# Convolution input, queries and gate of a hybrid RG-LRU and attention layer: from still to moving weights, turned by TensorE, with two attention lanes and a new order of column groups

## The chip, the cores and the metric

The kernel runs on one core of one Trainium2 chip. The metric is device time in microseconds (us), the median of several runs; lower is better. The engines named below are PE (TensorE: matrix products, with its weight loads as PEld), ACT (ScalarE), DVE (VectorE), POOL (GpSimd) and SP, whose queue issues the loads of the weights.

## The reference

One layer on 256 tokens of 2048 channels, all in float32:

```python
h = h + W_out [ norm(RG-LRU group) ; norm(NSA group) ]   # one RMSNorm, one combined input projection
h = h + ConvGatedMLP(RMSNorm(h))                          # then a final RMSNorm
# columns of the input projection w_in (2048 x 4632)
C_X, C_G, C_Q, C_KC, C_VC, C_KS, C_VS, C_KW, C_VW, C_BG = (
    0, 1024, 2048, 3072, 3328, 3584, 3840, 4096, 4352, 4608)
```

X (1024 columns) goes through a causal convolution of 4 taps to `u`; two products of `u` with 128x128 blocks per head give the gates r and i (sigmoids); with a = exp(-8 r softplus(-lambda)) the recurrence is h_t = a_t h_(t-1) + sqrt(1 - a_t^2) i_t u_t, and its result is multiplied by gelu(G), G being 1024 columns more. Q, K and V serve an attention of 8 query heads and 2 key heads with three branches: over compressed blocks (a small two-layer network with weights `cmp_w1` on K and V), over selected blocks, over a window. Both halves are normed and go through `w_out`.

## The kernel before

**Products.** Each float32 product is three products of the faster fp32r type: a weight is split into hi + lo, the activations too, and hi·hi, hi·lo and lo·hi are summed in PSUM. The weights stream through in parts of 128 x 1024 numbers (`PART`), two to a load of 1 MB on SP's queue (tile `raw`, 3 buffers). For each part ACT makes `hi` (L285) and DVE makes `lo` (L286); each of the two pools has 4 buffers. All that PE does for a part takes some 2.7 to 2.9 us.

**Three ways to multiply.** `mm_weights_still_plain` (L314) loads 128x128 of the weight into PE and moves 256 tokens through it, three matmuls of 256 columns (L323 to L325); the result has channels on partitions. `mm_weights_still` (L328) moves the activations' hi and lo side by side, 512 columns, for the weight's hi (L345) and 256 columns for its lo (L343); `halves` then adds the two halves of the result. `mm_weights_move` (L357) loads 128 tokens of the activations and moves up to 512 columns of the weight (L369 to L371); the result has tokens on partitions.

**Order.** `run_stream` (L290) walks a list of parts. The list is made of column groups: KC and VC by turns, KS, KW by turns with `cmp_w1_k`, Q's first 256 columns by turns with `cmp_w1_v`, then VW, Q, VS, Q, Q, four groups of 256 for X, four for G, four of 512 for `w_out` with the attention half, four with the LRU half, and then `w_up`, the convolution and `w_down` in three pieces. All of X, G, Q and K use `mm_weights_still_plain`. The code beside the products hangs in lanes (`Lane`, L57): each is a queue of generators, run whenever its due time has come, where the clock is counted in matrix steps (`PACE` a step of 256 columns). The tile framework then sets the order of each engine's queue.

**What the lanes do.** `norm_x` (L379) makes the scale of the first norm and then `blocks` (L425): the blocks of K and V for compression, on POOL (L427, L434), split by ACT (L436) and DVE (L437) into `kbs`. `post_q` (L508) scales the queries and adds two `attention` tasks, for tokens 0 to 127 and 128 to 255, to one lane. `post_lru_x` writes X to `xp`, and `lru` (L664) does convolution, gate products (L694 to L696) and tanh/exp for a pair of heads (ACT L698 to L702). When the last G group is done `recurrence` (L716) takes square roots (L725), scans (DVE L731), gelu of G (L734) and the product (L737), split for `w_out` by `two_parts` (L216).

Of the kernel before, what the change touches and what calls it, by code (L numbers as in the profile page):

```python
# [15 lines left out]
P = 128  # L16
# [62 lines left out]
def hymba_block(ctx, tc, x, g_mix, w_in, lru_conv_w, lru_conv_b, lru_wa, lru_ba, lru_wx, lru_bx, lru_lambda,  # L79
# [43 lines left out]
    mix = mixctx.enter_context(tc.tile_pool(name="mix", bufs=1))  # L123
    cmpp = cmpctx.enter_context(tc.tile_pool(name="cmpp", bufs=1))
# [91 lines left out]
    def two_parts(dst, src, gain=None):  # L216

        hi, lo = dst[:, 0], dst[:, 1]
        if gain is None:
            act(hi, src, AF.Copy)  # L220
            tt(lo, src, hi.bitcast(F32), op=OP.subtract)
        else:
            act(hi, src, AF.Copy, scale=gain)  # L223
            stt(lo, src, gain, hi.bitcast(F32), op0=OP.mult, op1=OP.subtract)  # L224

    def transpose_in(cg, g, dst):

        for pair in range(2):
            t = ps_t.tile([P, 512], F32, name="pt")
            for j in range(2):  # L230
                c = cg * 512 + (pair * 2 + j) * P
                for b in range(NB):
                    nc.tensor.transpose(t[:, j * S + b * P:j * S + (b + 1) * P], xr[:, b, c:c + P], ident)
            for j in range(2):
                i = pair * 2 + j
                two_parts(dst[:, i], t[:, j * S:(j + 1) * S], g(cg * 4 + i))
# [11 lines left out]
    lanes = {n: Lane() for n in ("x", "att", "lru", "gate")}  # L248
# [65 lines left out]
    def mm_weights_still_plain(src):  # L314

        def fn(p, j, k, st, kts):
            if k == 0:
                st["ps"] = ps_mm.tile([P, 2, 512], F32, name="mm")
            a = src(k)
            for m in range(2):  # L320
                o = st["ps"][:, m, :S]
                wh, wl = p.hi[:, j, m * P:(m + 1) * P], p.lo[:, j, m * P:(m + 1) * P]
                mm(o, lhsT=wh, rhs=a[:, 0], start=k == 0, stop=False)  # L323
                mm(o, lhsT=wh, rhs=a[:, 1], start=False, stop=False)  # L324
                mm(o, lhsT=wl, rhs=a[:, 0], start=False, stop=k == kts - 1)  # L325
        return fn

# [20 lines left out]
    def halves(dst, ps):  # L348

        t = ev.tile([P, 2, S], F32, name="ev")  # L350
        nc.scalar.copy(t, ps[:, :, S:])  # L351
        tt(dst, ps[:, :, :S], t, op=OP.add)  # L352

# [28 lines left out]
    def norm_x():  # L382
# [12 lines left out]
        rsq = cst.tile([P, S], F32, name="rsbq")  # L395
        nc.vector.tensor_scalar_mul(rsq, shared["rsb"], QSCALE)
        shared["rsbq"] = rsq
# [3 lines left out]
        blocks(0)  # L401
        yield 1000
        blocks(1)
# [13 lines left out]
    kbs = [cmpp.tile([P, CB, 2, KVH * NC], F32R, name=f"kbs{i}") for i in range(2)]  # L417
    NST = 4 * KVH * NC

    def post_cmp_in(which):  # L420
        def post(st):
            nc.vector.tensor_copy(kvc[:, which], st["ps"][:, :, :S])
        return post

    def blocks(which):  # L425

        nc.gpsimd.tensor_tensor(kvc[:, which], kvc[:, which], over_pair(shared["rsb"]), op=OP.mult)  # L427
        src = kvc[:, which].rearrange("p v (n l) -> p l v n", l=CS)
        kb = cmpp.tile([P, CB, KVH * NC], F32, name="kb")
        dst = kb.rearrange("p l (v n) -> p l v n", v=KVH)  # L430
        for half in range(2):
            for v in range(KVH):
                off = pe[:, which * CB + half * CS:which * CB + (half + 1) * CS]
                nc.gpsimd.tensor_tensor(dst[:, half * CS:(half + 1) * CS, v], src[:, :, v, half:half + NC],  # L434
                                        off.unsqueeze(2).to_broadcast([P, CS, NC]), op=OP.add)
        act(kbs[which][:, :, 0], kb, AF.Copy)  # L436
        tt(kbs[which][:, :, 1], kb, kbs[which][:, :, 0].bitcast(F32), op=OP.subtract)  # L437

# [15 lines left out]
    def post_cmp(which):  # L454
# [5 lines left out]
        def finish_cmp(ps):  # L460
# [15 lines left out]
            else:  # L476
# [7 lines left out]
                open_mixers()  # L484
        return post

    def post_keys(br):
        def post(st):
            tt(kcat[:, :, br], st["ps"][:, :, :S], over_pair(shared["rsb"]), op=OP.mult)
        return post  # L490

    ready = set()

    def post_values(br):
        def post(st):
            ready.add(br)
            for b in range(NB):
                src, rs = st["ps"][:, b, :256], shared["rs"][:, b:b + 1]
                act(vnat[0][:, b, br], src, AF.Copy, scale=rs)
                stt(vnat[1][:, b, br], src, rs, vnat[0][:, b, br].bitcast(F32), op0=OP.mult, op1=OP.subtract)  # L500
            if br == 1:

                for b in range(NB):
                    act(gates[:, b], st["ps"][:, b, 256:280], AF.Tanh, scale=shared["rsh"][:, b:b + 1])
                ts(gates, gates, 0.5, 0.5, op0=OP.mult, op1=OP.add)
        return post

    def post_q(i):  # L508
        def post(st):
            tt(qT[:, 2 * i:2 * i + 2], st["ps"][:, :, :S], over_pair(shared["rsbq"]), op=OP.mult)  # L510
            if i % 2 == 1:
                yA.append(split_new())
                for b in range(NB):
                    lanes["att"].add(attention(i // 2, b))
        return post

# [8 lines left out]
    def open_mixers():  # L525
        late["at"] = mixctx.enter_context(tc.tile_pool(name="at", bufs=1))
        late["lr"] = mixctx.enter_context(tc.tile_pool(name="lr", bufs=1))
# [23 lines left out]
    def attention(g, b):  # L551
# [13 lines left out]
        pc = at.tile([P, GQA, NC], F32, name="pc")  # L565
# [11 lines left out]
        pr = at.tile([P, GQA, 2, S], F32, name="pr")  # L577
# [13 lines left out]
        yield 1000  # L591
        nc.vector.reciprocal(cf, tot)
# [19 lines left out]
        for n, step in enumerate(steps):  # L612
# [5 lines left out]
            pT = [at.tile([P, 512], F32R, name=f"pT{n % 2}{i}") for i in range(2)]  # L618
# [8 lines left out]
        sq = at.tile([P, 512], F32R, name="pT00").bitcast(F32)  # L627
        act(sq, o, AF.Square)
        for h in range(GQA):
            two_parts(yA[g][:, h, :, qs], o[:, h * P:(h + 1) * P], g_att(g * GQA + h))  # L630
# [21 lines left out]
    lru_sq = cst.tile([P, S], F32, name="lru_sq")  # L652
    halfway = []
    gated = []

    def post_lru_x(i):
        def post(st):
            xp = late["lr"].tile([P, 2, S + 3], F32, name="xp")
            nc.gpsimd.memset(xp[:, :, 0:3], 0.0)
            tt(xp[:, :, 3:], st["ps"][:, :, :S], over_pair(shared["rsb"]), op=OP.mult)  # L660
            lanes["lru"].add(lru(i, xp))
        return post

    def lru(i, xp):  # L664
        lr = late["lr"]
# [6 lines left out]
        e = lr.tile([P, 2, S], F32, name=f"gt{i}")  # L672
# [7 lines left out]
        for m in range(2):  # L680
            t = 2 * i + m
            nc.gpsimd.tensor_scalar(u[:, m], xp[:, m, 0:S], conv_w(0, t), conv_b(t), op0=OP.mult, op1=OP.add)
# [25 lines left out]
    def post_lru_g(i):  # L708
        def post(st):
            gt = late["lr"].tile([P, 2, S], F32, name=f"gt{i}")  # L710
            tt(gt, st["ps"][:, :, :S], over_pair(shared["rsb"]), op=OP.mult)
            gated.append(gt)
            if i == 3:
                lanes["lru"].add(recurrence())
        return post

    def recurrence():
        room = scratch_new()
        ms = [room[:, :, h] for h in range(2)]
        for m, w in zip(ms, halfway):  # L720
            stt(m, w[:, :, 0], 2.0, w[:, :, 0], op0=OP.subtract, op1=OP.mult)
            nc.gpsimd.tensor_scalar(w[:, :, 0], w[:, :, 0], -1.0, 1.0, op0=OP.mult, op1=OP.add)
        yield 2600
        for m in ms:
            act(m, m, AF.Sqrt, scale=-0.25)  # L725
        yield 1500
        for m, w in zip(ms, halfway):
            tt(w[:, :, 1], w[:, :, 1], m, op=OP.mult)
            yield 1500
            for j in range(4):  # L730
                nc.vector.tensor_tensor_scan(m[:, j], w[:, j, 0], w[:, j, 1], 0.0, op0=OP.mult, op1=OP.add)  # L731
            yield 2000
        for gt in gated:
            act(gt, gt, AF.Gelu_apprx_tanh)  # L734
        yield 2000
        for i, gt in enumerate(gated):
            tt(gt, gt, ms[i // 2][:, (i % 2) * 2:(i % 2) * 2 + 2], op=OP.mult)  # L737
            if i % 2 == 0:
                yL.append(split_new())
            for m in range(2):  # L740
                two_parts(yL[i // 2][:, (i % 2) * 2 + m], gt[:, m], g_lru(2 * i + m))
            yield 1500
            for m in range(2):
                if i == 0 and m == 0:
                    nc.gpsimd.tensor_tensor(lru_sq, gt[:, 0], gt[:, 0], op=OP.mult)
                else:
                    nc.gpsimd.tensor_tensor(gt[:, m], gt[:, m], gt[:, m], op=OP.mult)
                    nc.gpsimd.tensor_tensor(lru_sq, lru_sq, gt[:, m], op=OP.add)
            yield 1000
        yield 5000  # L750
        shared["rsL"] = channel_rms(lru_sq, "rsL")
# [50 lines left out]
    def post_up_v(t0):  # L802
        def post(st):
# [7 lines left out]
            two_parts(aT[t0 // 4][:, i % 4:i % 4 + 2].rearrange("p k a s -> p a k s"), v)  # L811
# [74 lines left out]
    group(wi, C_KS, 256, KT, still_x, post_keys(0))  # L886
    with_cmp = lambda g, w, which: by_turns(g, group(w[0], 0, P, CB, mm_cmp(which), post_cmp(which), cuts=[8] * (CB // 8)))
    with_cmp(group(wi, C_KW, 256, KT, still_x, post_keys(1), cuts=halves_of), cmp_w1_k, 0)
    still_q = lambda i, cuts=None: group(wi, C_Q + i * 256, 256, KT, still_x, post_q(i), cuts=cuts)
    with_cmp(still_q(0, halves_of), cmp_w1_v, 1)  # L890
    group(wi, C_VW, 280, KT, move_x, post_values(1))
    still_q(1)
    group(wi, C_VS, 256, KT, move_x, post_values(0))
    still_q(2)
    still_q(3)
    for i in range(4):
# [50 lines left out]
```

## Time and profile before

| | |
|---|---|
| median of 3 runs | 1178.77 us (1178.74 to 1179.24) |
| profiled execution, its own time | 1178.34 us |
| span in its trace | 1176.6 us, so 1.74 us lie outside it |
| busy: PE, DVE, ACT, POOL | 1160.9, 778.6, 589.7, 159.8 us |
| chain that ended last: PE, DVE | 91%, 2% |
| input projection and mixers | about the first 280 of the 1176.6 us |

Busy times say how long an engine was at work in all; the chain follows back from the last instruction what released each step. Matmuls overlap one another on PE, so their step from start to start is what one costs, and not the duration of one.

### The profile page before, as it was taken

The numbers are of one execution on the slowest core, as the hardware profiler recorded it, in microseconds if no ns is written. First come the engines' busy times: TensorE is split into PE (matmuls) and PEld (weight loads), VectorE is DVE, ScalarE is ACT, GpSimd is POOL, SyncE is SP. The second block draws the span as 40 slices with busy tenths as digits, with TensorE's granted clock in tenths as the row PEclk, the third lists the DMA queues.
The fourth block names the chain that finished last, engine by engine and source line by source line (L and its number), as shares of the span: only waits on it lengthen the run. The fifth ranks groups of instructions, "written<-read, shape, count | busy, mean of one in ns | idle before, by whom it ended". The sixth has DMA issues, their size and how long they took to land.

```text
span 1176.6 us, 16684 instructions
## 1 busy us (share of the span) xinstructions
PE 1160.9 (99%) x6727; PEld 1021.8 (87%) x6727; DVE 778.6 (66%) x981; ACT 589.7 (50%) x803; POOL 159.8 (14%) x181
## 2 busy tenths in 40 slices
PE   8999999999999999999999999999999999999997
PEld 7999999898788888888888888888888888888885
DVE  5775778779766676677455676677455677677554
ACT  5554546687446554444333455444333445445444
POOL 3210224123300110110000110110000110110000
PEclk8999999999999999999999999999999999999999
DMA  9676545443655565565555565565555565565561
GB/s 297 180 222 215 159 126 156 135 150 139 214 191 177 176 206 181 180 210 184 188 205 181 181 210 181 179 203 190 184 209 180 179 210 183 179 198 189 189 207 76
DMA packets 182397, 217.60 MB, mean 185 GB/s; under 512 B 4064, under 2 KB 147584, under 8 KB 182192
## 3 DMA queue, kind: packets, MB, share of 16 engines
q1 hardware_dynamic: 180928, 213.07, 55.4%
q0 software_dynamic: 1072, 2.41, 0.6%
q8 instruction: 52, 0.85, 0.4%
q10 hardware_dynamic: 320, 1.06, 0.2%
q14 instruction: 25, 0.20, 0.1%
HBM read 214.43 MB, written 2.10 MB: 184 GB/s over the span
## 4 chain that ended last, share of the span: by engine, by line
PE 91%; DVE 2%; ACT 0%; issue 0%; POOL 0%; DVEq 0%
PE mm L345 30%; PE mm L343 16%; PE mm L370 9%; PE mm L371 9%; PE mm L369 9%; PE mm L325 4%; PE mm L323 4%; PE mm L324 4%; PE s L582 1%; DVE lo L286 1%; PE s L371 1%; PE s L369 1%; PE s L370 1%; PE pt L617 1%; DVE act L224 0%; PE s L608 0%
## 5 line engine op out<-in xcount | busy, mean ns | idle before, releaser
L286 DVE TENSOR_TENSOR lo<-raw,hi 128x1024 fp32r<-128x1024 f32 (+1 forms) x403 | 527.6, 1316 | 248.2 <-ACT hi L285 248.1
L285 ACT ACTIVATE hi<-raw 128x1024 fp32r<-128x1024 f32 (+1 forms) x403 | 423.9, 1054 | 397.0 <-PE mm L371 183.4
L345 PE MATMUL mm<-act,hi 128*128 128x512 f32 x1536 | 367.7, 391 | 0.0
L345 PEld LDWEIGHTS mm<-act,hi 128*128 128x128 f32 x1536 | 282.1, 188 | 54.3
L370 PE MATMUL mm<-lo,act 128*128 128x512 f32 (+2 forms) x544 | 206.0, 379 | 2.1 <-DVE lo L286 2.1
L371 PE MATMUL mm<-hi,act 128*128 128x512 f32 (+2 forms) x544 | 205.7, 378 | 0.0
L369 PE MATMUL mm<-hi,act 128*128 128x512 f32 (+2 forms) x544 | 205.6, 378 | 0.0
L343 PEld LDWEIGHTS mm<-act,lo 128*128 128x128 f32 x1536 | 197.3, 191 | 7.7
L343 PE MATMUL mm<-act,lo 128*128 128x256 f32 x1536 | 199.8, 283 | 0.0
L323 PE MATMUL mm<-act,hi 128*128 128x256 f32 x512 | 147.1, 290 | 2.5 <-ACT act L223 1.7
L325 PE MATMUL mm<-act,lo 128*128 128x256 f32 x512 | 147.8, 289 | 0.1
L324 PE MATMUL mm<-act,hi 128*128 128x256 f32 x512 | 146.8, 288 | 0.4 <-DVE act L224 0.4
L370 PEld LDWEIGHTS mm<-lo,act 128*128 128x128 f32 x544 | 102.2, 188 | 22.4 <-DVE lo L286 3.8
L369 PEld LDWEIGHTS mm<-hi,act 128*128 128x128 f32 x544 | 102.2, 188 | 19.0 <-issue 0.4
L371 PEld LDWEIGHTS mm<-hi,act 128*128 128x128 f32 x544 | 102.2, 188 | 18.8
L356 POOL TENSOR_TENSOR up<-up,rsb 128x512 f32<-128x512 f32 x24 | 29.6, 1234 | 587.7 <-DVE up L352 503.6
L323 PEld LDWEIGHTS mm<-act,hi 128*128 128x128 f32 x512 | 98.3, 193 | 5.4 <-issue 2.1
L325 PEld LDWEIGHTS mm<-act,lo 128*128 128x128 f32 x512 | 98.7, 193 | 2.8 <-issue 1.8
L324 PEld LDWEIGHTS mm<-act,hi 128*128 128x128 f32 x512 | 98.7, 193 | 2.2 <-issue 1.2
L351 ACT COPY ev<-mm 128x512 f32<-128x512 f32 x48 | 28.2, 587 | 125.8 <-PE mm L345 125.8
L352 DVE TENSOR_TENSOR up<-mm,ev 128x512 f32<-128x512 f32 x24 | 16.6, 692 | 49.5 <-ACT ev L351 49.5
L356 POOL TENSOR_TENSOR cv<-cv,rsb 128x512 f32<-128x512 f32 x24 | 38.0, 1582 | 20.8 <-ACT cv L797 20.8
(238 smaller groups left out, 737.9 us busy)
## 6 DMA issues: line engine op xcount, KB each, us to landing
raw<-in_w_up_dram SPq DMA_DIRECT2D x96, 1024.0 KB, 5.2
raw<-in_w_down_dram SPq DMA_DIRECT2D x48, 1024.0 KB, 5.1
raw<-in_w_in_dram SPq DMA_DIRECT2D x26, 1024.0 KB, 5.5
raw<-in_w_out_dram SPq DMA_DIRECT2D x16, 1024.0 KB, 5.0
raw<-in_w_in_dram SPq DMA_DIRECT2D x15, 512.0 KB, 4.6
xr<-in_x_dram SPq DMA_DIRECT2D x4, 512.0 KB, 7.6
raw<-in_cmp_w_k_dram SPq DMA_DIRECT2D x4, 512.0 KB, 5.7
raw<-in_cmp_w_v_dram SPq DMA_DIRECT2D x4, 512.0 KB, 5.4
```

The source lines that it names most:

```text
L285: act(hi[:, :n], src, AF.Copy)
L286: tt(lo[:, :n], src, hi[:, :n].bitcast(F32), op=OP.subtract)
L323: mm(o, lhsT=wh, rhs=a[:, 0], start=k == 0, stop=False)
L324: mm(o, lhsT=wh, rhs=a[:, 1], start=False, stop=False)
L325: mm(o, lhsT=wl, rhs=a[:, 0], start=False, stop=k == kts - 1)
L343: mm(o[:, S:], lhsT=w, rhs=a[:, 0], start=False, stop=False)
L345: mm(o, lhsT=w, rhs=a.rearrange("p a s -> p (a s)"), start=kk == 0, stop=kk == kts - 1)
L351: nc.scalar.copy(t, ps[:, :, S:])
L356: nc.gpsimd.tensor_tensor(a, a, over_pair(shared[rs]), op=OP.mult)
L369: keep(mm(o, lhsT=h, rhs=p.hi[:, j], start=k == 0, stop=False))
L370: mm(o, lhsT=h, rhs=p.lo[:, j], start=False, stop=False)
L371: mm(o, lhsT=l, rhs=p.hi[:, j], start=False, stop=k == kts - 1)
```

## The change

It has five parts. (1) `mm_weights_still_plain` is gone: KC, VC, KS and KW use `mm_weights_still`, with `halves` behind it. (2) X, Q and G are six groups of 512 columns with the weights moving. Their results have tokens on partitions, so ACT copies them to `tok` with the norm's scale (`by_token`), and PE turns them back with 128x128 transposes (`turned`), 8 to a group. (3) The two attention tasks of a group of heads run in two lanes (`att0`, `att1`). (4) The group order is KC/VC, X0, KS with `cmp_w1_k`, KW with `cmp_w1_v`, Q0, VW, VS, Q1, X1, G0, G1, then `w_out` as before. (5) `blocks` runs on DVE; the LRU's first convolution tap and the sign change of the recurrence move from POOL to ACT; the pool `lr` has one buffer of each tile (`tok`, `xp`, `u`, ...), which `recurrence` and `gate` take over from `lru`; square roots are done for each pair and gelu reads the transposes from PSUM.

```diff
-    still_x, move_x = mm_weights_still_plain(tiles_of(xT)), mm_weights_move(tiles_of(xT))
+    still_x, move_x = mm_weights_still(tiles_of(xT)), mm_weights_move(tiles_of(xT))
...
-        nc.gpsimd.tensor_tensor(kvc[:, which], kvc[:, which], over_pair(shared["rsb"]), op=OP.mult)
+        tt(kvc[:, which], kvc[:, which], over_pair(shared["rsb"]), op=OP.mult)
...
+    def by_token(st, rs):
+        tok = lr.tile([P, NB, 512], F32, name="tok")
+        for b in range(NB):
+            act(tok[:, b], st["ps"][:, b], AF.Copy, scale=shared[rs][:, b:b + 1])
+        return tok
+    def turned(tok, pair):
+        t = ps_t.tile([P, 512], F32, name="pt")
+        for j in range(2):
+            c = (pair * 2 + j) * P
+            for b in range(NB):
+                nc.tensor.transpose(t[:, j * S + b * P:j * S + (b + 1) * P], tok[:, b, c:c + P], ident)
+        return t.rearrange("p (j s) -> p j s", j=2)
...
+    def recurrence():
+        room = [lr.tile([P, 2, S], F32, name="u")]
...
+            act(w[:, :, 0], w[:, :, 0], AF.Identity, scale=-1.0, bias=1.0)
+            yield 700
+        for m in room:
+            act(m, m, AF.Sqrt, scale=-0.25)
...
+    def gate(cg, tok):
+        while len(scanned) < 4:
+            yield PACE
+        yield 1300
+        turns = [turned(tok, pair) for pair in range(2)]
...
+        for gt, t in zip(gts, turns):
+            act(gt, t, AF.Gelu_apprx_tanh)
...
-    group(wi, C_KS, 256, KT, still_x, post_keys(0))
+    wide = lambda c0, post: group(wi, c0, 512, KT, move_x, post)
+    wide(C_X, post_lru_x(0))
+    with_cmp(group(wi, C_KS, 256, KT, still_x, post_keys(0), cuts=halves_of), cmp_w1_k, 0)
...
-    for i in range(4):
-        group(wi, C_G + i * 256, 256, KT, still_x, post_lru_g(i))
+    wide(C_X + 512, post_lru_x(1))
+    for cg in range(2):
+        wide(C_G + cg * 512, post_lru_g(cg))
```

Three places show how the change moves instructions. The first is ACT's queue at the beginning of `w_out`. Before, it holds the last splits (`hi`), the gelu of G (L734), the two square roots (L725), and then a run of splits:

```order
L285 ACTIVATE hi<-raw 128x1024
L734 ACT_TABLE_LOAD
L734 ACTIVATE gt_3187<-gt_3187 128x512
L285 ACTIVATE hi<-raw 128x1024
L725 ACT_TABLE_LOAD
L725 ACTIVATE act<-act 128x4x256 x2
L285 ACTIVATE hi<-raw 128x1024 x4
```

At the same place of the queue after the change the square roots (L748) and the gelu (L765) alternate with the last pair's exp and tanh (L726, L727), each with a load of the function table; `wg` and `u` are the taken-over buffers, L745 is the sign change, L493 the copy of the second G group to `tok`:

```order
L748 ACT_TABLE_LOAD
L748 ACTIVATE u_2495<-u_2495 128x512
L727 ACT_TABLE_LOAD
L727 ACTIVATE act<-act,sp_591 128x256
L286 ACTIVATE hi<-raw 128x1024
L726 ACTIVATE xp<-act,sp4n 128x256
L745 ACTIVATE act<-act 128x2x256
L748 ACT_TABLE_LOAD
L748 ACTIVATE u_2494<-u_2494 128x512
L765 ACT_TABLE_LOAD
L765 ACTIVATE wg_2621<-pt 128x512
L493 ACTIVATE tok<-mm,rs 128x512 x2
```

From the split of the fourth `w_out` part to that of the ninth, 5 splits now share ACT's queue with 8 table loads; before, the last square roots stand ahead of a run of 4 splits.

The second place is PE's queue where G1 ends and `w_out` begins (L361 to L363 are the moving matmuls, L719 to L721 the gate products of the third pair of heads, L502 the transposes of the fourth). After the change:

```order
L719 MATMUL pt<-u_2244,wg_2246 128x256
L720 MATMUL pt<-u_2245,wg_2246 128x256
L721 MATMUL pt<-u_2244,wg_2247 128x256
L502 MATMUL pt<-ident,tok 128x128 x4
L665 MATMUL pt<-ones,att_sq 128x1 x2
L361 MATMUL mm<-hi,act 128x512
L362 MATMUL mm<-lo,act 128x512
L363 MATMUL mm<-hi,act 128x512
```

The fourth pair of heads is turned only here, just ahead of the first matmul of `w_out`; the fourth pair's gate products and both G tiles' transposes follow among the `w_out` parts.

The third place is the making of the blocks for compression. Before, it is on POOL:

```order
L427 TENSOR_TENSOR kvc<-kvc,rsb 128x512 x2
L434 TENSOR_TENSOR kb<-kvc,pe 128x16x15 x8
```

After the change it is in DVE's queue between the splits (L287):

```order
L419 TENSOR_TENSOR kvc<-kvc,rsb 128x512 x2
L427 TENSOR_TENSOR kb<-kvc,pe 128x16x15 x4
L287 TENSOR_TENSOR lo<-raw,hi 128x1024 x2
L433 TENSOR_TENSOR act<-kb,act 128x32x30
L427 TENSOR_TENSOR kb<-kvc,pe 128x16x15 x4
```

The blocks left POOL's queue, and the eight X0 parts now lie between KC/VC and the first use of the blocks.

## Rows read from the trace of the kernel before

**Rows 1.** The page: its span, busy times, and the chain by engine

```profile
span 1176.6 us, 16684 instructions
...
PE 1160.9 (99%) x6727; PEld 1021.8 (87%) x6727; DVE 778.6 (66%) x981; ACT 589.7 (50%) x803; POOL 159.8 (14%) x181
...
PE 91%; DVE 2%; ACT 0%; issue 0%; POOL 0%; DVEq 0%
```

**Rows 2.** Windows: us, busy PE, PEld, DVE, ACT, POOL, granted clock, DMA share, GB/s

```profile
371.20:1176.60 805.40, 796.93 (x4237) 689.48 (x4235) 513.90 (x569) 372.06 (x439) 78.00 (x76) 1.00 0.56 186
...
238.00:272.00 34.00, 34.00 (x267) 32.36 (x267) 25.50 (x42) 29.29 (x45) 5.58 (x10) 1.00 0.55 181
272.00:300.00 28.00, 26.11 (x131) 20.86 (x130) 28.00 (x33) 16.42 (x22) 13.72 (x15) 1.00 0.34 119
```

**Rows 3.** Waits of PE over the span: total us, times, longest us

```profile
PE mm L370 <- DVE lo L286: 2.1, 4, 0.9
...
PE mm L323 <- ACT hi L285: 0.8, 1, 0.8
PE s L450 <- ACT hi L285: 0.4, 1, 0.4
```

**Rows 4.** Timeline of DVE from 276 us: start us, us, instruction

```profile
277.29 4.75 DVE L731 TENSOR_TENSOR_SCAN act<-act 128x256 f32<-128x256 f32 x8
281.96 1.20 DVE L286 TENSOR_TENSOR lo<-raw,hi 128x1024 fp32r<-128x1024 f32 x1
```

**Rows 5.** The chain in 59 to 70 us: start us, us, what

```profile
63.00 2.35 POOL kb L434 x2
...
65.37 1.03 ACT kbs L436
```

**Rows 6.** The chain at 269, 341 and 387 us: start us, us, what

```profile
269.93 0.12 PE mm L324
...
272.93 0.12 PE mm L325
...
341.53 0.66 PE pt L233 x6
...
387.46 3.67 PE mm L345 x16
391.13 1.91 PE mm L343 x16
```

**Rows 7.** Timeline of PE at 280 and 341 us: start us, us, instruction

```profile
280.18 0.39 PE L370 MATMUL mm<-lo,act 128*128 128x512 f32 x1
...
282.68 0.39 PE L369 MATMUL mm<-hi,act 128*128 128x512 f32 x1
...
341.94 0.48 PE L369 MATMUL mm<-hi,act 128*128 128x512 f32 x1
```

**Rows 8.** Timeline of ACT from 254.2 us: start us, us, instruction

```profile
254.19 0.47 ACT L699 ACTIVATE act<-pt,vh 128x256 f32<-128x256 f32 x1
254.67 1.28 ACT L701 ACT_TABLE_LOAD   x1
255.97 0.60 ACT L701 ACTIVATE gt<-act,sp4n 128x256 f32<-128x256 f32 x1
256.47 0.58 ACT L628 ACTIVATE pT<-s 128x512 f32<-128x512 f32 x1
256.95 0.36 ACT L223 ACTIVATE act<-s,vec 128x128 fp32r<-128x128 f32 x1
257.20 0.60 ACT L702 ACTIVATE act<-act,sp 128x256 f32<-128x256 f32 x1
257.69 0.47 ACT L698 ACTIVATE act<-pt,vh 128x256 f32<-128x256 f32 x1
...
258.41 1.07 ACT L285 ACTIVATE hi<-raw 128x1024 fp32r<-128x1024 f32 x1
259.36 0.38 ACT L223 ACTIVATE act<-s,vec 128x128 fp32r<-128x128 f32 x1
```

More of the change, by code (lines that the diff above doesn't have):

```diff
@@ L247, in hymba_block @@
     parts = []
-    lanes = {n: Lane() for n in ("x", "att", "lru", "gate")}
+    lanes = {n: Lane() for n in ("x", "q", "att0", "att1", "lru", "gate")}
     def group(w, c0, ncols, kts, mm_fn, post, cuts=None, row0=0):
@@ L312, in hymba_block @@
     on_load = {}
[L314 to L326, printed above, removed]
     def mm_weights_still(src):
@@ L416, in hymba_block @@
     w2 = cmpp.tile([P, 2, P], F32, name="w2")
-    kbs = [cmpp.tile([P, CB, 2, KVH * NC], F32R, name=f"kbs{i}") for i in range(2)]
+    kbs = []
     NST = 4 * KVH * NC
@@ L504, in post, with post_q, queries @@
                     act(gates[:, b], st["ps"][:, b, 256:280], AF.Tanh, scale=shared["rsh"][:, b:b + 1])
+            for b in range(NB):
+                stt(vnat[1][:, b, br], st["ps"][:, b, :256], shared["rs"][:, b:b + 1], vnat[0][:, b, br].bitcast(F32),
+                    op0=OP.mult, op1=OP.subtract)
+            if br == 1:
                 ts(gates, gates, 0.5, 0.5, op0=OP.mult, op1=OP.add)
         return post
-    def post_q(i):
+    def post_q(g):
         def post(st):
[L510 to L514, printed above, removed]
-        return post
+            lanes["q"].add(queries(g, by_token(st, "rsq")))
+        return post
+    def queries(g, tok):
+        for pair in range(2):
+            yield 1300
+            h = g * GQA + pair * 2
+            act(qT[:, h:h + 2], turned(tok, pair), AF.Copy)
+        yA.append(split_new())
+        for b in range(NB):
+            lanes[f"att{b}"].add(attention(g, b))
     yA, yL = [], []
@@ L652, in hymba_block, with post_lru_x, lru @@
     lru_sq = cst.tile([P, S], F32, name="lru_sq")
+    scanned = []
     halfway = []
-    gated = []
-    def post_lru_x(i):
+    def post_lru_x(cg):
         def post(st):
[L658 to L661, printed above, removed]
-        return post
-    def lru(i, xp):
-        lr = late["lr"]
+            tok = by_token(st, "rs")
+            for pair in range(2):
+                lanes["lru"].add(lru(2 * cg + pair, tok, pair))
+            if cg == 1:
+                lanes["lru"].add(recurrence())
+        return post
+    def lru(i, tok, pair):
+        while "vh" not in late:
+            yield PACE
+        yield 1300
+        xp = lr.tile([P, 2, S + 3], F32, name="xp")
+        nc.gpsimd.memset(xp[:, :, 0:3], 0.0)
+        act(xp[:, :, 3:], turned(tok, pair), AF.Copy)
         if i % 2 == 0:
@@ L706, in lru, with post_lru_g @@
         yield 1300
-    def post_lru_g(i):
+    def post_lru_g(cg):
         def post(st):
[L710 to L714, printed above, removed]
+            lanes["gate"].add(gate(cg, by_token(st, "rs")))
         return post
     def recurrence():
-        room = scratch_new()
-        ms = [room[:, :, h] for h in range(2)]
-        for m, w in zip(ms, halfway):
+        room = [lr.tile([P, 2, S], F32, name="u")]
+        room += [lr.tile([P, 2, S], F32R, name=f"u{n}").bitcast(F32) for n in range(2)]
+        room.append(lr.tile([P, 2, 2, P], F32R, name="wg0").bitcast(F32).rearrange("p a b e -> p a (b e)"))
+        mine = [halfway[i // 2][:, (i % 2) * 2:(i % 2) * 2 + 2] for i in range(4)]
+        for m, w in zip(room, mine):
```

141 lines of the change are left out of this document (70 added, 71 removed).

## The prediction

> **What bounds the kernel now.** I read the page first: PE is busy for 1160.9 of 1176.6 us, and the chain that ended last runs through PE for 91% of the span [rows 1]. So time can come from two things only: from what PE has to do, and from the stretches in which it stands still. From 371 us on PE is at work for 796.93 of 805.40 us at full clock [rows 2], and the change touches nothing there. What matters lies in the first 300 us. There I read PE's waits: in 2.1 us, in four pieces, it waits for `lo` from DVE in moving matmuls, and in 1.2 us for `hi` from ACT, once in a projection and once in the compression [rows 3]. Then the windows: in 238 to 272 us, where the last recurrences are prepared, PE is busy without a break (34.00 of 34.00) although ACT is busy for 29.29; in 272 to 300, at the beginning of `w_out`, DVE is busy for all 28.00 us and PE for 26.11 [rows 2]. The timeline of DVE shows why: eight scans take it from 277.29 to 281.96 without a split between them [rows 4]. The chain shows the other stall: at 63 us POOL makes `kb`, ACT's `kbs` follows at 65.37, and the splits behind it in ACT's queue come late [rows 5].
>
> **PE's own work.** Prices are steps from start to start. A plain matmul of 256 columns costs 0.120 us (25 steps between 269.93 and 272.93), a hi matmul of 512 columns with its lo of 256 costs 0.349 (16 of each, 3.67 + 1.91), a transpose 0.11 (6 in 0.66) [rows 6]; a moving matmul of 512 columns costs 0.2273 (11 steps from 280.18 to 282.68) [rows 7].
> - KC, VC, KS and KW: 96 plain matmuls a group, 11.52 us, become 32 pairs, 11.16 us. Four groups save 1.4.
> - X, Q and G: for 512 columns 192 plain matmuls (23.04 us) become 96 moving ones (21.82 us). Six groups save 7.3.
> - Six groups add 8 transposes each, 48 x 0.11 = 5.3. Behind a batch of transposes a matmul lasts 0.48 us where 0.39 is usual [rows 7]; ten batches (two gate tiles count once each) cost 0.9.
>
> The net is 2.5 us less. That is the whole gain in arithmetic: turning the tiles back eats most of what the moving form saves.
>
> **Stalls that go.** At the beginning of `w_out`, 2.1 us of waits [rows 3]. Each break also loses the overlap of two matmuls, 0.39 - 0.227 = 0.16 us [rows 7], so 2.7 with four breaks. I take it away whole, because the eight scans no longer stand in a row on DVE, and put whatever takes its place into the new stall below. The waits behind `kbs`, 1.2 us and two breaks, 1.5: the blocks now run on DVE with eight X0 parts, some 22 us, between KC/VC and their first use. If that cover failed, the 1.5 would be back. Together 4.2 us.
>
> **Small burst at KS and KW.** There ACT gains `halves` for each key group, the copies of X0 to `tok` and LRU work of the first X. Nothing to 1.3 us (the size of the old stall there); I take 0.5, since in the window with ACT busy for 29.29 of 34.00 us PE stood unbroken [rows 2]. The other edits cost PE nothing: two attention lanes change when matmuls come, not how many, and POOL's work that moved to ACT and DVE is covered but for the place that follows.
>
> **The new stall.** X1 comes seven groups after X0, G0 and G1 directly behind it, and the LRU lane does the pairs of heads one after the other with one `xp`, one `u` and one `tok`. In PE's queue the fourth pair is turned only ahead of the first `w_out` matmul, so its gates, all square roots, the scans and both gelu tiles fall into the first eight `w_out` parts. I count ACT's queue from behind the split of the fourth `w_out` part to the end of the split of the ninth, with the steps of [rows 8]:
> - 5 splits at 0.95 (258.41 to 259.36): 4.75
> - 8 table loads at 1.30 (254.67 to 255.97): 10.4
> - 14 instructions of 512 columns at 0.48 (256.47 to 256.95): 6.7
> - 8 tanh from PSUM at 0.36 (257.69 to 258.41 for two): 2.9
> - 10 instructions of 256 columns with a scale per partition at 0.50 (255.97 to 256.47): 5.0
> - 2 copies of 256 columns, 0.4 each as an estimate between these two: 0.8
> - 5 of 128 columns or fewer at 0.25 (256.95 to 257.20): 1.25
>
> That is 31.8 us. In the same stretch PE has, from its first `w_out` matmul to its ninth part, 96 moving matmuls (21.8), 12 gate products of 256 columns (1.4) and 12 transposes (1.3), 24.5 us. How early can ACT begin? There are four `hi` buffers, so the fourth `w_out` split waits until PE is through with G1's last part. Between that and `w_out` PE has 12 gate products, 3 attention matmuls and 4 transposes, 2.5 us, of which the split takes 0.95. So ACT starts 1.6 us ahead of PE and is 31.8 - 24.5 - 1.6 = 5.7 us too late with the ninth split, even if it never waits.
>
> It will wait. The convolution's six steps on DVE stand between ACT's first tap and its copy of `u`; `xp` is free for the fourth pair only when DVE has read `e` of the third; each square root waits for a product on DVE. The bound below is nothing. For the bound above I take ACT without any overlap of its instructions: they last about 0.1 longer than their steps (0.60 against 0.50, 0.58 against 0.48, 1.07 against 0.95) [rows 8], for the 44 beside the loads 4.4. I take 2.5, as about half of them hand over to another engine. Last, the transposes of the second G tile need a PSUM tile that the first tile's second gelu has to read, and this gelu stands behind the ninth and tenth splits and a table load. PE's queue has these transposes just behind the first matmul of the ninth part: another 0.95 + 1.30 + 0.48 = 2.7 us. The waits for the `tok` copies of G0, whose PSUM tile holds up `w_out`, lie inside the same delay. Sum: 5.7 + 2.5 + 2.7 = 10.9 us of new standstill, between 2 (if the waits and the late gelu are hidden, and two thirds of the 5.7 by a start of ACT that is earlier than I can see) and 15.5 (5.7 + 4.4 + 2.7, and the 2.7 of the old stall behind DVE's scans, if it comes back).
>
> **A rule against it.** ACT's load at 254.67 starts 0.01 us after L699 has ended at 254.66, and the next instruction comes 1.30 us later [rows 8]: nothing is paid beside the load. The Trainium skill, "ScalarE: Activation LUTs", section "What ACT_TABLE_LOAD costs", gives 1283 ns for the load and some 1380 ns of drain beside it, 2.66 us a switch; by that page the eight loads would cost 11 us more. The first of its two figures agrees with the trace (1.28), the second doesn't show there.
>
> **Sum.** 1178.3 (the profiled execution, 0.4 below the median of the runs) - 2.5 - 4.2 + 0.5 + 10.9 = 1183.0.
>
> **Rivals.**
> - ScalarE's burst is hidden (stall of 2 or less): 1178.3 - 6.7 + 0.5 + 2 = 1174, faster. For it: before, 29.29 us of ACT in 34 stopped PE not at all [rows 2]. Against it: 31.8 us are now to fit in 26.1. It decides below a stall of 4.3 us; from there on the kernel is no longer faster by over 0.2%. Chance 0.22.
> - In between, a stall of 3 to 8 us, if PE's waits overlap so that the gelu's 2.7 and the waits on DVE vanish: 1175 to 1180. Chance 0.18.
> - VectorE becomes the bound with ScalarE, each waiting for the other's whole duration in convolution, square root, scan and product: 15.5 us of standstill by the upper ends above, with 1.3 at KS and KW 1188.6, and 1186 to 1190 around it. For it: in 272 to 300 us DVE was busy for 28.00 of 28.00 already [rows 2], and it now gets the blocks' and recurrence's work more finely interleaved. Chance 0.13.
> - Each switch of ACT's table also drains the engine, on eight loads that PE waits for: 8 x 1.38 longer, 1194. Rows 8 speak against it. Chance 0.03.
>
> **Chances and range.** My forecast, a stall of 8 to 14 us (1180 to 1186), has 0.44. Of this kernel 0.2% (2.4 us) is about what a measurement can tell from no change: faster is below 1176.4, slower above 1181.1. Faster takes the first rival and a quarter of the second: 0.26. The same takes the rest of the second and a little of the forecast: 0.20. Slower 0.54. The range 1173 to 1190 leaves out the better part of the first rival's low side and the last one, about 0.15; the forecast's own range is 1180 to 1186.
>
> **What would show it.** In the changed kernel: a window of the first eight `w_out` parts in which ACT is busy nearly all the time and PE for some 70%; PE's waits there named `hi` (L286), the gelu (L765) and the copy to `tok` (L493), and no wait near `kbs`; still pairs at 0.349, moving matmuls at 0.227 and transposes at 0.11; the first matmul of `w_out` some 4 us earlier than before. It would be wrong if the fourth pair's transposes ran before G1's parts, if PE's waits there came to less than 5 us, or if new waits showed in the attention, where two lanes now share the PSUM buffers.

## The result and the profile after

The changed kernel takes 1184.86 us in the median of 4 runs (1183.86 to 1185.84), the kernel before 1179.01 (4 runs): ratio 1.0052, 95% interval 1.004 to 1.0065. It is slower by about 6 us, where 1183 was forecast. The profiled execution took 1185.45 us with a span of 1183.7. The page, against [rows 1]:

```profile
span 1183.7 us, 15395 instructions
...
PE 1161.7 (98%) x6071; PEld 991.9 (84%) x6071; DVE 772.5 (65%) x985; ACT 615.0 (52%) x849; POOL 126.5 (11%) x153
...
PE 97%; ACT 2%; DVE 0%; DMA 0%; issue 0%; SPq 0%
```

PE has 656 instructions fewer, ACT 25 us more to do, and ACT appears in the chain where DVE stood. The waits of PE over the span (total, times, longest) say where, against [rows 3]:

```profile
PE mm L332 <- DVE act L227: 2.5, 1, 2.5
PE mm L361 <- ACT hi L286: 2.4, 1, 2.4
PE pt L502 <- ACT xp L765: 2.3, 1, 2.3
PE pt L665 <- ACT act L724: 2.3, 1, 2.3
...
PE pt L502 <- ACT tok L493: 1.0, 1, 1.0
...
PE mm L361 <- DVE xr L797: 0.4, 1, 0.4
PE pt L502 <- ACT act L724: 0.2, 1, 0.2
```

The two old waits are gone. The six last lines of these, 8.6 us, all lie between 268 and 308 us, at the beginning of `w_out`; the first is the very first matmul of the projection. The windows (us, busy PE, PEld, DVE, ACT, POOL, granted clock, DMA share, GB/s), against [rows 2]:

```profile
60.00:100.00 40.00, 40.00 (x254) 36.12 (x253) 36.23 (x49) 32.31 (x48) 0.10 (x1) 1.00 0.81 240
...
266.00:268.00 2.00, 2.00 (x12) 1.50 (x12) 1.23 (x1) 1.73 (x4) 0.21 (x1) 1.00 0.10 36
268.00:272.00 4.00, 1.74 (x12) 1.53 (x10) 2.25 (x6) 4.00 (x12) 2.10 (x6) 0.84 0.74 238
272.00:277.70 5.70, 5.62 (x14) 4.35 (x15) 3.14 (x10) 3.40 (x8) 0.11 (x1) 0.52 0.50 201
277.70:284.00 6.30, 6.30 (x30) 5.21 (x29) 4.35 (x10) 4.95 (x7) 0.00 (x0) 1.00 0.00 0
...
300.00:310.00 10.00, 5.30 (x19) 3.79 (x18) 7.11 (x10) 9.93 (x11) 0.00 (x0) 0.74 0.02 3
```

At KS and KW, 60 to 100 us, PE never stops. From 300 to 310 us ACT is busy for 9.93 of 10 us and PE for 5.30. And the row of 272.00 to 277.70 shows something that my sum didn't have: PE is busy for 5.62 of 5.70 us at a granted clock of 0.52, that is at 1.2 GHz nearly throughout. The timeline of PE there (start us, us, instruction):

```profile
268.24 0.60 PE L502 MATMUL pt<-ident,tok 128*128 128x128 f32 x4
271.10 0.99 PE L665 MATMUL pt<-ones,att_sq 128*128 128x1 f32 x4 [2.26 <-ACT act L724]
272.17 0.80 PE L361 MATMUL mm<-hi,act 128*128 128x512 f32 x1
272.76 0.63 PE L362 MATMUL mm<-lo,act 128*128 128x512 f32 x1
...
277.46 0.42 PE L361 MATMUL mm<-hi,act 128*128 128x512 f32 x1
277.72 0.40 PE L362 MATMUL mm<-lo,act 128*128 128x512 f32 x1
```

From 268.84 to 272.17 PE does nothing but four matmuls of one column. Behind this break the moving matmuls step by 0.43 us (11 between 272.76 and 277.46) and not by 0.227; 13 steps from 272.17 take 5.55 us where 2.95 would do, 2.6 us lost. After 307 us eight more such steps lose 1.7. For 2.26 us of the break the trace names ACT's L724, a tanh that reads the PSUM tile that the four small matmuls need; the first `w_out` matmul then starts at 272.17, just behind the end of ACT's two copies to `tok` (L493, 270.80 to 272.12). The timeline of ACT ahead of the second pair of waits:

```profile
299.71 1.28 ACT L748 ACT_TABLE_LOAD   x1
301.01 0.63 ACT L748 ACTIVATE u<-u 128x512 f32<-128x512 f32 x1
301.66 1.28 ACT L727 ACT_TABLE_LOAD   x1
302.95 0.60 ACT L727 ACTIVATE act<-act,sp 128x256 f32<-128x256 f32 x1
303.46 1.99 ACT L286 ACTIVATE hi<-raw 128x1024 fp32r<-128x1024 f32 x2
305.46 1.28 ACT L765 ACT_TABLE_LOAD   x1
306.76 0.60 ACT L765 ACTIVATE xp<-pt 128x512 f32<-128x512 f32 x1
```

This is the place that the prediction counted: the ninth split (303.46) stands behind a square root and a tanh with a table load each, and the gelu that frees PE's PSUM tile (306.76) behind the tenth split and a load more. ACT has 11 table loads between 255 and 330 us. The Trainium skill, "ScalarE: Activation LUTs", section "What ACT_TABLE_LOAD costs", adds a drain of some 1380 ns to each load; the step from 301.66 to 302.95 is 1.29 us with the load in it, so no drain shows here either.

### The profile page after: what moved, and what is told of

It is laid out like the page before. It is cut to its first block, busy times and chain, and to the rows that moved or that the text cites. A ratio compares the mean times of both kernels' runs of the same rounds, so it can differ in the third digit from the quotient of the medians.

```text
span 1183.7 us, 15395 instructions
## 1 busy us (share of the span) xinstructions
PE 1161.7 (98%) x6071; PEld 991.9 (84%) x6071; DVE 772.5 (65%) x985; ACT 615.0 (52%) x849; POOL 126.5 (11%) x153
## 4 chain that ended last, share of the span: by engine, by line
PE 97%; ACT 2%; DVE 0%; DMA 0%; issue 0%; SPq 0%
PE mm L332 32%; PE mm L330 17%; PE mm L361 14%; PE mm L362 14%; PE mm L363 14%; PE s L600 1%; PE s L447 1%; PE pt L637 1%; PE s L363 1%; PE s L361 1%; PE s L362 1%; PE pt L236 0%; DMA raw<-in_w_in_dram 0%; PE s L628 0%; PE pt L502 0%; PE s L629 0%
## 5 line engine op out<-in xcount | busy, mean ns | idle before, releaser
L287 DVE TENSOR_TENSOR lo<-raw,hi 128x1024 fp32r<-128x1024 f32 (+2 forms) x403 | 523.5, 1306 | 253.2 <-ACT hi L286 252.4
L286 ACT ACTIVATE hi<-raw 128x1024 fp32r<-128x1024 f32 (+2 forms) x403 | 423.8, 1054 | 365.1 <-PE mm L363 201.9
L332 PEld LDWEIGHTS mm<-act,hi 128*128 128x128 f32 x1664 | 306.3, 189 | 61.5 <-DVE act L227 2.7
L361 PE MATMUL mm<-hi,act 128*128 128x512 f32 (+2 forms) x736 | 284.0, 386 | 2.9 <-ACT hi L286 2.4
L363 PE MATMUL mm<-hi,act 128*128 128x512 f32 (+2 forms) x736 | 284.0, 386 | 0.0
L362 PE MATMUL mm<-lo,act 128*128 128x512 f32 (+2 forms) x736 | 283.9, 386 | 0.0
L330 PEld LDWEIGHTS mm<-act,lo 128*128 128x128 f32 x1664 | 214.9, 191 | 9.2 <-DVE lo L287 0.8
L330 PE MATMUL mm<-act,lo 128*128 128x256 f32 x1664 | 219.1, 283 | 0.6 <-DVE lo L287 0.6
L361 PEld LDWEIGHTS mm<-hi,act 128*128 128x128 f32 x736 | 139.5, 190 | 31.2 <-ACT hi L286 2.9
L363 PEld LDWEIGHTS mm<-hi,act 128*128 128x128 f32 x736 | 139.3, 189 | 27.6 <-issue 1.2
L362 PEld LDWEIGHTS mm<-lo,act 128*128 128x128 f32 x736 | 139.4, 189 | 27.3 <-issue 1.4
L348 POOL TENSOR_TENSOR cv<-cv,rsb 128x512 f32<-128x512 f32 x24 | 38.3, 1595 | 21.5 <-ACT cv L829 21.5
L339 DVE TENSOR_TENSOR v<-mm,ev 128x512 f32<-128x512 f32 x24 | 16.6, 691 | 35.7 <-ACT ev L338 35.7
L828 DVE SCALAR_TENSOR_TENSOR cv<-up,fvec,cv 128x256 f32<-128x256 f32 x48 | 20.8, 472 | 0.0
L827 DVE SCALAR_TENSOR_TENSOR cv<-up,fvec,cv 128x256 f32<-128x256 f32 x48 | 20.8, 471 | 0.0
```

What stands on the lines that cost most here:

```text
L286: act(hi[:, :n], src, AF.Copy)
L287: tt(lo[:, :n], src, hi[:, :n].bitcast(F32), op=OP.subtract)
L330: mm(o[:, S:], lhsT=w, rhs=a[:, 0], start=False, stop=False)
L332: mm(o, lhsT=w, rhs=a.rearrange("p a s -> p (a s)"), start=kk == 0, stop=kk == kts - 1)
L348: nc.gpsimd.tensor_tensor(a, a, over_pair(shared[rs]), op=OP.mult)
L361: keep(mm(o, lhsT=h, rhs=p.hi[:, j], start=k == 0, stop=False))
```

## The experiments

**Taking the table loads away.**

```diff
-            act(m, m, AF.Sqrt, scale=-0.25)
+            act(m, m, AF.Copy, scale=-0.25)
...
-            act(gt, t, AF.Gelu_apprx_tanh)
+            act(gt, t, AF.Tanh)
```

> The changed kernel with the recurrence's square root replaced by a scaled copy and the gate's gelu by tanh, so that ACT needs no other function table for them; the result is not the layer's. All other instructions stay in the same order. Theory (ScalarE's queue at the beginning of w_out is what PE waits for): six table loads of 1.28 us between the fourth and the ninth split go, and the gelu's own, so the ninth split and the second G tile's transposes come some 8 to 9 us earlier; the waits from 297 us on (1.2, 2.6 and 2.6 us) and the 1.2 GHz behind them (8 matmuls at 0.43, 1.6 us) vanish, while the first break at 269 us (2.4 us and 13 matmuls at 0.43) stays: 1184.9 - 8 = 1177, between 1175 and 1179. Rival (VectorE's products and scans and the hand-overs set the pace, the loads fill ACT's waits): less than 3 us are won, 1182 or more.

1174.66 us (1174.38 to 1176.95), ratio to before 0.9973 (0.9963 to 0.9984): 10 us less than the changed kernel where 8 were expected, with the same instructions in the same order on ACT otherwise. PE's waits from 255 us on:

```profile
PE pt L665 <- ACT act L724: 2.3, 1, 2.3
PE mm L361 <- ACT tok L493: 0.5, 1, 0.5
PE mm L361 <- DVE xr L797: 0.4, 1, 0.4
```

The break at 268 us stays, the waits for `hi` and the gelu are gone, and so are the slow steps behind them. The theory holds in its mechanism; VectorE's share was not what PE waited for. Its size is less sure: of the 10.8 us between the two profiled executions 1.2 lie ahead of 38 us, where the two kernels do not differ (see part 1 below), and 0.9 in fewer slow steps behind the first break.

**Keeping the square roots, under one load.**

```diff
-            act(m, m, AF.Sqrt, scale=-0.25)
+            tc.keep_in_program_order(act(m, m, AF.Sqrt, scale=-0.25))
```

> The changed kernel with the recurrence's four square roots held behind the last pair's exp and tanh on ACT, so that one table load serves all four; everything is computed. Five table loads are left of eleven between the fourth w_out part and the second G tile. Theory (the loads on ACT's queue are what PE waits for from 297 us on): 1184.9 - 8 = 1177, between 1175 and 1179, with no step of 0.43 us behind 300 us. Rival (the later square roots delay scans and gates, and PE's transposes and w_out's second half wait for them): 1181 or more.

1178.01 us (1176.63 to 1180.89), ratio 0.9999 (0.999 to 1.0008): as fast as the kernel before, some 7 us better than the changed one. ACT has 5 loads where it had 11. The wait for `hi` is gone; 1.2 us for `lo` takes its place at 311 us (waits of PE from 255 us on, then a window behind this wait):

```profile
PE pt L665 <- ACT act L724: 2.3, 1, 2.3
PE mm L362 <- DVE lo L287: 1.2, 1, 1.2
PE mm L361 <- DVE xr L797: 1.0, 2, 0.6
```

```profile
312.00:316.00 4.00, 3.98 (x11) 3.20 (x12) 4.00 (x6) 3.18 (x4) 2.12 (x1) 0.58 0.69 229
```

That there would be no step of 0.43 us behind 300 us did not come true: behind waits of 0.6 and 1.2 us with one matmul between them, eight steps from 312.02 to 315.51 lose 1.7 us. The profiled execution, 1180.85 us, is one of the two slowest of the 11.

**The order: the second X group early.**

```diff
     wide(C_X, post_lru_x(0))
+    wide(C_X + 512, post_lru_x(1))
...
-    wide(C_X + 512, post_lru_x(1))
```

> The changed kernel with one line moved: the second X group directly behind the first, so that all four pairs of heads and the square roots are done before w_out. Theory (what costs is that the recurrence falls into w_out's first parts): the standstill there, 9.9 us of waits and 4.2 us at 1.2 GHz in the changed kernel, shrinks to what the two gelu tiles need, 1 to 3 us, without a fall of the clock: 1184.9 - 12 = 1173, between 1170 and 1175. Rival 1 (the work is too much for ScalarE wherever it lies: it runs into KS and KW, where the compression already burdens it): as many waits at 60 to 130 us as go at 270 to 310, 1180 or more. Rival 2 (the moving form and its transposes cost more than their steps): the waits go and the time stays above 1178.

1193.89 us (1193.12 to 1194.96), ratio 1.0135 (1.0121 to 1.0149). My theory missed by 21 us. The recurrence was indeed out of `w_out`'s first parts, but the compression, with X1's parts and the LRU's work ahead of it, has its last matmuls (L476) at 166 us and not at 116, the attention's first scores (L600) come at 178 and not at 129, and of the groups only G0 and G1 are left to cover its second half. PE's longest waits from 260 us on:

```profile
PE pt L665 <- POOL lru_sq L779: 3.2, 1, 3.2
PE mm L361 <- DVE xr L797: 2.0, 1, 2.0
PE s L628 <- ACT pT L639: 1.4, 2, 1.2
PE pt L502 <- ACT wg L765: 1.4, 1, 1.4
```

In 268 to 292 us PE was busy for 18.65 of 24 us at a granted clock of 0.79. X1 stands behind Q1 in the changed kernel because X1 is also the attention's cover. Rival 1 was right that the cost moves; it named the wrong place, and of the 10.4 us that PE waits from 260 us on only 3.7 are for ACT.

**The lanes.**

```diff
-            lanes[f"att{b}"].add(attention(g, b))
+            lanes["att0"].add(attention(g, b))
```

> The changed kernel with the two attention tasks of a group in one lane again. Theory (the two lanes are what lets the second group's attention end before w_out in the new order): scores of the second group still stand in PE's queue where w_out begins, so the w_out parts wait for attention and ACT gets its exponentials into the same burst: 1190 or more. Rival (lanes move matmuls and cost or save nothing): 1185 within 2.

1198.13 us (1197.2 to 1199.74), ratio 1.0168 (1.0154 to 1.0182). As expected, and worse: PE waits for the attention's probabilities (`pr`) from 267.9 to 279.7 us, where `w_out` should begin.

```profile
PE pt L637 <- DVE pr L617: 11.7, 1, 11.7
```

The new group order needs the second lane: without it the changed kernel is 13 us slower. My prediction had put the lanes at nothing; no run tries them in the old order.

**The engine of the blocks.**

```diff
-        tt(kvc[:, which], kvc[:, which], over_pair(shared["rsb"]), op=OP.mult)
+        nc.gpsimd.tensor_tensor(kvc[:, which], kvc[:, which], over_pair(shared["rsb"]), op=OP.mult)
...
-                tt(dst[:, half * CS:(half + 1) * CS, v], src[:, :, v, half:half + NC],
+                nc.gpsimd.tensor_tensor(dst[:, half * CS:(half + 1) * CS, v], src[:, :, v, half:half + NC],
```

> The changed kernel with the blocks for compression back on POOL. Theory (eight X0 parts lie between KC/VC and the first use, so the engine that makes the blocks no longer matters): 1184.9 within 1 us. Rival (the move to DVE is what took the old wait behind kbs away): that wait comes back, 1.2 us and two breaks, 1186.4.

1186.2 us (1184.81 to 1187.07), ratio 1.0068 (1.0055 to 1.0081). The intervals overlap that of the changed kernel, so the time alone decides nothing. But the waits at 55 to 90 us, of which the changed kernel has none, are plain (`kbs` lies in `act` now, L447 uses it; 0.3 us more is at L330):

```profile
PE s L447 <- ACT hi L286: 0.5, 1, 0.5
PE s L447 <- DVE lo L287: 0.4, 1, 0.4
```

As to the waits the rival holds: 1.2 us of them are back, with eight X0 parts ahead of it POOL's chain still comes too late, and it was the move to DVE that took the wait away.

**Part 1 undone, and part 1 carried further.** For both the groups' form is exchanged: the changed kernel with `mm_weights_still_plain` and no `halves`, and the kernel before with `mm_weights_still` and `halves` for all sixteen groups.

```diff
-    still_x, move_x = mm_weights_still(tiles_of(xT)), mm_weights_move(tiles_of(xT))
+    still_x, move_x = mm_weights_still_plain(tiles_of(xT)), mm_weights_move(tiles_of(xT))
```

> The changed kernel with part 1 undone: KC, VC, KS and KW with plain matmuls of 256 columns, and no halves to add. Theory (four groups cost PE 0.36 us more each, the additions were covered): 1184.9 + 1.4 = 1186.3, between 1185.5 and 1187. Rival (the wide form at the very start and the additions cost what it saves): 1184.9 or less.

1183.51 us (1181.63 to 1185.19), ratio 1.0042 (1.003 to 1.0053), whose interval overlaps that of the changed kernel: part 1 brings nothing that can be measured here. The start is one place where its 1.4 us are lost. Timelines of PE, first with part 1 undone:

```profile
7.94 0.58 PE L324 MATMUL mm<-act,hi 128*128 128x256 f32 x1 [1.42 <-ACT act L221]
```

then the changed kernel:

```profile
8.99 1.22 PE L332 MATMUL mm<-act,hi 128*128 128x512 f32 x2 [2.50 <-DVE act L227]
```

A matmul over both parts of the activations has to wait for DVE's part as well, 1.05 us later. But the second plain matmul (L325) waits for DVE too, until 8.82 us, so this alone is not the cost. The first matmul of X0, behind KC and VC, shows more; here the changed kernel's, then that of the second try with two `tok` buffers, which starts in the same way:

```profile
38.16 0.48 PE L361 MATMUL mm<-hi,act 128*128 128x512 f32 x1
35.44 0.48 PE L362 MATMUL mm<-hi,act 128*128 128x512 f32 x1
```

In ten profiled executions with the wide form at the start it comes at 35.4 to 38.3 us, on the whole the later the lower the granted clock was in 10 to 15 us (1.00 down to 0.50). With part 1 undone it came at 37.30 at a clock of 0.56 (wide: 38.16 at 0.53) and, in the last run below, at 36.45 at 0.76 (wide: 36.95 at 0.75). So at a like clock the wide form reached X0 0.5 to 0.9 us later, where the sum had it 0.7 earlier. And two profiled executions can differ by 2.9 us before any other edit acts.

> The kernel before with one part of the change, and more of it: all sixteen groups with the weights at rest (KC, VC, KS, KW, Q, X, G) use the form with 512 and 256 columns, their two halves added by ACT and DVE; nothing is turned, order and lanes as before. Theory (a group costs PE 11.16 instead of 11.52 us, and the additions are covered): 16 x 0.36 = 5.8 us less than before, 1179.0 - 5.8 = 1173.2, between 1172 and 1175, and the two old waits (2.1 us for lo, 1.2 for hi) as before. Rival (ACT's copy and DVE's addition hold the PSUM tile and delay the splits, 16 times): the waits grow by more than 3 us, 1176 or more.

1192.88 us (1191.38 to 1193.43), ratio 1.0124 (1.011 to 1.0137), where 1173 was expected. PE's waits:

```profile
PE mm L374 <- DVE xr L770: 5.1, 1, 5.1
PE mm L345 <- DVE act L224: 3.4, 3, 1.9
PE mm L375 <- DVE lo L286: 3.0, 3, 1.9
PE mm L343 <- DVE lo L286: 1.9, 2, 1.7
```

In 294 to 318 us DVE was busy for 23.34 of 24 us. No addition of halves lies in that window; the last one starts at 290.70, and what DVE does there is work that has come late: the second four scans start at 299.35, where before all eight were done by 282.04 [rows 4], and the scale that L770 needs, for which PE waits 5.1 us (`rsA`), is ready only at 312.4, behind them. DVE has 7.7 us more to do than before in all, ACT 8.2: one more pass over each result on each of them. That this is what made DVE late is argued, since no run takes it away from DVE alone. If so, a cheaper matmul form is paid for by the engines that empty PSUM. That is what the wide, moving form of X, Q and G avoids: it has no halves to add.

**Two buffers for `tok`.** The first try took room from `u`:

```diff
+    tokp = mixctx.enter_context(tc.tile_pool(name="tokp", bufs=2))
...
-        tok = lr.tile([P, NB, 512], F32, name="tok")
+        tok = tokp.tile([P, NB, 512], F32, name="tok")
...
-        u = lr.tile([P, 2, S], F32, name="u")
+        u = ev.tile([P, 2, S], F32, name="ev")
```

> The changed kernel with two buffers for tok (u and the squares' throw-away output share the buffer of halves to make room). Theory 1 (the first break at 269 us comes from the one tok: G0's copy waits for the fourth pair's transposes, and G0's PSUM tile holds up w_out): the break of 2.3 and the rest up to 272.2, and the 13 matmuls at 0.43 behind it, go. Theory 2 (but ACT's queue as a whole sets when the ninth part starts): PE then waits longer at 297 to 307 us, and only 1 to 4 us are won, 1181 to 1184. Rival (the breaks are independent): the whole 5.7 us, 1179.

1185.63 us (1183.69 to 1185.93), ratio 1.0058 (1.0045 to 1.007). The total says that nothing was won, the trace says that two things happened. In 270 to 290 us PE was busy for 19.55 of 20 us at full clock, so the first break is gone; but in 90 to 105 us it was busy for 8.92 of 15 at 0.65, because KS's and KW's `halves` now wait for `u` in the same buffer. Their additions (L340) start at 102.3 and 104.4 us; in the second try below, with `u` apart, at 74.0 and 90.9. PE stands with the LRU's and the compression's matmuls alone in its queue:

```profile
PE pt L472 <- ACT hT L468: 3.1, 1, 3.1
PE pt L720 <- ACT u L711: 1.6, 1, 1.6
PE pt L721 <- DVE u L712: 1.4, 1, 1.4
```

> Both together: two tok buffers, and the square roots under one table load. Theory: with ACT's queue shorter by 8 us and the first break gone, PE has no wait over 1 us between 260 and 320 us and no step at 1.2 GHz: 1184.9 - 8 - 5.7 = 1171, between 1169 and 1174, faster than the kernel before. Rival (the first break only moves, because PE then reaches the gelu earlier than ACT does): 1175 or more.

1185.61 us (1183.94 to 1186.61), ratio 1.006 (1.0048 to 1.0073): from 260 to 320 us PE is busy for 59.42 of 60 us at full clock, as expected, but the same new wait at 90 to 105 us takes it back, and nothing is added to the run before. A second try leaves `u` alone and puts one of the attention's `pT` tiles in that buffer, which KS and KW have left by then:

```diff
-            pT = [at.tile([P, 512], F32R, name=f"pT{b}{i}") for i in range(2)]
+            pT = [at.tile([P, 512], F32R, name=f"pT{b}{i}") if (b, i) != (1, 1) else
+                  ev.tile([P, 2, S], F32, name="ev").rearrange("p a s -> p (a s)").bitcast(F32R) for i in range(2)]
```

> Two tok buffers again, with u in a buffer of its own as in the changed kernel: the room comes from one of the attention's pT tiles and the squares' throw-away output, which share the buffer of halves. Theory (the 11 us of waits at 91 to 103 us in the last try came only from u sharing a buffer with halves; its first break was gone): 1185.6 - 11 = 1175, between 1172 and 1177, faster than the kernel before, and no step of 0.43 us at the beginning of w_out. Rival (PE, arriving earlier, waits for ACT's queue as much as is gained): 1181 or more.

1174.68 us (1172.97 to 1175.91), ratio 0.9966 (0.9954 to 0.9978): faster than both kernels. Its windows and PE's waits from 255 us on:

```profile
260.00:280.00 20.00, 19.56 (x95) 15.39 (x94) 12.24 (x22) 13.75 (x26) 2.42 (x7) 1.00 0.54 192
280.00:300.00 20.00, 19.86 (x98) 16.60 (x97) 18.08 (x31) 17.06 (x27) 0.00 (x0) 1.00 0.48 159
...
310.00:320.00 10.00, 7.66 (x32) 5.67 (x32) 10.00 (x15) 5.31 (x8) 1.18 (x2) 1.00 0.48 147
```

```profile
PE mm L363 <- DVE lo L288: 1.6, 1, 1.6
PE mm L364 <- DVE act L228: 1.2, 2, 0.8
PE mm L362 <- ACT hi L287: 0.8, 1, 0.8
```

8.6 us of waits have become 3.6, of which 2.8 are for DVE (busy for 10.00 of 10 us at 310 to 320) and 0.8 for ACT, and the granted clock is 1.00 all through 255 to 340 us. This execution, 1172.97 us, is the fastest of the five; its start had the full clock. With two buffers both halves of a G tile are there together, so the schedule also comes out with 6 table loads in 255 to 330 us in place of 11.

> The same with the four square roots under one table load, that is one load fewer in the part of ACT's queue that PE waits for. Theory (with two tok buffers the loads are no longer what PE waits for, since the list of ACT's queue differs by one or two loads there): the same as with two tok buffers alone within 1.5 us. Rival (each load counts): 3 us less, 1172.

1174.96 us (1173.35 to 1175.98), ratio 0.9966 (0.9953 to 0.9978): no different, with 5 loads. The second buffer leaves nothing for the grouping to win, as it would be if both remove the same lateness of ACT's queue.

> Two tok buffers together with part 1 undone (plain matmuls for KC, VC, KS and KW). Theory (the wide form loses at the very start, where its first matmul waits for both parts of the activations and the clock stays at 1.2 GHz longer, what it saves later): within 1.5 us of two tok buffers alone, 1173 to 1176, and the first matmul of the projection half a microsecond earlier. Rival (the 1.4 us that undoing part 1 gave were real): 1173.3 or less.

1174.69 us (1173.81 to 1175.7), ratio 0.9968 (0.9956 to 0.9981). The total is as the theory said, so the 1.4 us that undoing part 1 seemed to give are within the spread. The first matmul starts at 8.11 and not at 8.86 us. A clock that stays low for longer with the wide form doesn't show: in 10 to 15 us it was 0.76 here and 1.00 in the profiled execution with two buffers alone.

## Why the prediction was right, and where its terms were off

- **PE's work.** PE has 656 instructions fewer; the 2.5 us were not measured by themselves. Of their 1.4 for part 1 nothing is seen (the run with part 1 undone, and that with two buffers beside it): the sum left out the start, where the wide form reaches X0 0.5 to 0.9 us later at a like clock.
- **Stalls that go.** Both went. The reason for `kbs` was half wrong: I named DVE and the X0 parts as cover, and the run with POOL shows that the X0 parts are not enough. The move to DVE counted.
- **KS and KW.** 0.5 us was forecast; PE is busy for 40.00 of 40.00 us there, so it is nothing.
- **The new stall.** Its stretch (the first `w_out` parts), its engine and its cause held: ACT's queue and its table loads, shown by the run without them. In size, 10.9 us of standstill was forecast. Measured are 8.6 us of waits with 6 breaks of 0.16, 9.6 us. I had the wait for the `tok` copies lie within the same delay; it stands apart, at 268.8 to 272.2 us, and vanishes with a second `tok` buffer. The gelu's own wait was 2.3 us for a forecast of 2.7.
- **Where the delay fell.** ACT needed 37.9 us from the end of the fourth split (266.60) to that of the ninth (304.5), for a forecast of 31.8 + 2.5. PE, free from 268.84 on, came to the ninth part's first matmul at 304.55: 35.7 us for 24.5 of work, 11.2 us late where 5.7 + 2.5 = 8.2 were forecast. But only 2.4 of them are a wait for the ninth split; 3.3 lie in the break ahead of the first matmul, 2.6 in slow steps, the rest in small waits. So the cause held and the delay was larger by 3 us, but the sum put nearly all of it at the ninth split, where little of it was seen.
- **What the sum lacked** is the clock: 2.6 + 1.7 = 4.3 us of steps at 1.2 GHz behind the two long breaks. 9.6 + 4.3 = 13.9 us in place of 10.9 is the term that was mis-sized, and most of why 1184.9 came out and not 1183. With 13.9 and nothing at KS and KW the sum gives 1178.3 - 2.5 - 4.2 + 13.9 = 1185.5, the profiled execution 1185.45; since a start can differ by 2.9 us, an agreement that close is luck.

The forecast's side, its mechanism and its range held. The rival that ScalarE's burst would be hidden fell; so did the one that VectorE becomes the bound with it, whose 1188.6 is 1188.4 by its own terms.

Of the signs, the first matmul of `w_out` came 5.0 us earlier (277.21 before, 272.17 after) for a forecast of 4, and the waits had the forecast's names. From that matmul to the ninth part PE was busy for 28.33 of 32.38 us, 87% and not 70%, as slow steps count as busy. And one sign of being wrong came in part: the longest wait of the first break is the attention's sum of squares (L665) at a PSUM tile, which the prediction didn't have.

What stays open: with ACT's lateness gone, 3.6 us of waits are left behind DVE and ACT, 0.4 at 273 us and the rest at 312 to 324, and no run took them away. Nor did any run put the first convolution tap and the sign change back on POOL, or undo the moving form alone, so what these cost ACT's queue is known from the count only.

## What to carry to other kernels

A matmul form that saves PE 0.3 us a group is worth it only if the engines that empty PSUM have that time to spare where the result falls due; here the saving was 2.5 us by the sum, and the work that it moved made PE wait for three times as much. Count, for the engine whose queue carries the splits, what stands between two of them, table loads first: eleven loads or five decided between 1185 and 1178. And a single buffer between two stages can hold a PSUM tile hostage far from where it is declared, so look for who frees it before adding work elsewhere. Where the room for a second buffer comes from matters as much: taken from `u` it won nothing, taken from `pT` some 10 us.

## What the hardware showed that was not expected

In the changed kernel the granted clock fell to 1.2 GHz after two breaks of PE, one of 3.3 us with four matmuls of one column in it, the other of two waits of 2.4 and 2.3 us with one part's first matmul between them; the slow steps behind them lasted until 277.5 and 311.5 us. With the roots under one load it fell after waits of no more than 0.6 and 1.2 us, with one matmul between them. Single waits of 0.8 and 1.6 us (two `tok` buffers, 310 to 330 us) and of up to 0.9 us [rows 3] left it at 1.00. So a wait can cost more than itself, namely a few microseconds of steps at 0.43 instead of 0.227 us behind it, and in the changed kernel this was 4.3 of some 14 us.

The start is not the same in every execution either: ten profiled executions that begin with the same products had a granted clock of 0.50 to 1.00 in 10 to 15 us and reached X0 between 35.4 and 38.3 us. A difference of 2 us between two single profiles may be no more than that.
